# A hybrid encoder block on one core: other PSUM banks, an earlier weight load, another first cast and 16 products moved

## The chip, the cores and the metric

The kernel runs on one core of a Trainium2 chip. TensorE (PE in the profile; PEld is its weight load) does the matmuls into PSUM; VectorE (DVE), ScalarE (ACT) and GpSimd (POOL) do the rest; SyncE (SP) and POOL issue the DMAs. Each engine works through its own instructions in order and waits on semaphores for the others. The metric is the device time of one execution in microseconds (us).

## What is computed

One layer of a streaming encoder over 512 frames of width 1024, in float32:

```
h = rmsnorm(x, norm_mix_g)
a_q, a_k, a_v, b_q, b_f, b_i, b_g, c_q, c_kv, c_kr, gate_logits = split(h @ w_in)
y_a = chunked_relpos_attention(a_q, a_k, a_v, rel_bias)
y_b = hgrn2_recurrence(b_q, b_f, b_i, b_g, lower_bound, norm_g)
y_c = mla_attention(c_q, c_kv, c_kr, positions, ...)
x = x + sum_n(sigmoid(gate_n) * (y_n @ w_branch[n])) @ w_out
h2 = rmsnorm(x, norm_ffn_g)
x = x + square(relu(h2 @ w_ff1)) @ w_ff2
return rmsnorm(x, final_norm_g)
```

Branch C (`mla_attention`) compresses the input to 256 + 128 + 32 columns, normalizes two of the parts, and expands them to queries, keys and values. Branch A has 8 heads of 64 with a relative bias. Branch B is a gated linear recurrence.

## The kernel before

Tensors lie transposed, features on the 128 partitions and the 512 frames along the free axis. Matmuls keep float32 accuracy by splitting both operands into a high half that TensorE takes as it is and a low half, the rest: one product of blocks is three matmuls, high by high, high by low, low by high (`mm3`, `mm3_u`). The norm of the input is applied late: `xg` holds x times the norm's gain, in halves, and each projection is multiplied by `rstd` as it leaves PSUM.

**The start.** `_body` first does eight steps k over 128 rows of x. A step makes the halves of x (ACT L400, VectorE L401), those of the compression weight `w_c` (`split`, L210 and L211), and adds 12 matmuls to four PSUM accumulators `pc` (L224 to L226). The squares of x (ACT L417) are summed by POOL (L419) into `ss`. Then the four accumulators are copied out as `crw` (ACT L427, VectorE L425), squared (L486), and summed over the partitions by matmuls with ones (L490 `pkv`, L491 `pst`, L492 `pq`). From these VectorE and ACT compute the norms (L496 to L506, `rsqrt`), `rstd` among them, and the halves of the normalized compression (`csplit`: `cnh`, `cnl`). The first value blocks `pv` of branch C need these (L635). PSUM has eight banks, given out by tags: `acc` three, `sc` two, `tp` two, `up` one.

**The filler.** While such chains run, TensorE is given matmuls of the large projections from a queue: `project` and `project_nat` add a function each, and `fill(n)` takes n units from it, one matmul of 512 columns each in `project` and on average the same in `project_nat`. TensorE's order is the order of the program (`manual_schedule`); that of the other engines is made by a planner from priorities, in program order, and estimated readiness. `TUNE` holds the sizes of the fills: `s0` ahead of L490, `s1` behind the norms, `c0`, `c1`, `c2`, `ca`, `cb` and `cd` in branch C's preparation, its attention and the attention's drain. The queue of this stage holds the eight blocks of `w_aqk` (24 matmuls each) and the two halves of `w_av`; branch B's projections are added behind the attention (L723).

**The weight loads.** `load` takes the next 512 KB block and issues its DMA on POOL into a buffer of tag `wr` (two buffers) or `wh` (three), by the count of loads so far modulo 5; at most two blocks wait unconverted. `convert` lets ACT write the negated high half to a `wl` buffer (three) and then POOL issues a second DMA of the same block that adds the full weight to it: the low half (L277, L278). `get`, called when a block's first matmul is due, makes sure that two blocks are converted, and asks for the next conversion 12 units later. The compression uses the same buffers: `w_c` comes in through `wr` in four tiles, and its halves lie in `wh` and `wl`, one tile for two steps. At the other end `stream`, for the output projection and the feed-forward part, takes over the three tags.

**Branch C's attention.** `attention` goes through 8 heads by 4 blocks of queries: scores, softmax, transposes two steps later, values; `ca` and `cb` fill between them, and four more rounds without scores drain it. The preparation of branch A's first heads (`prep_a`, L796 to L806) comes behind it in the program.

Of the kernel before, what the change touches and what calls it, by code (L numbers as in the profile page):

```python
# [9 lines left out]
F32 = mybir.dt.float32  # L10
F32R = mybir.dt.float32r
I32 = mybir.dt.int32
AF = mybir.ActivationFunctionType
ALU = mybir.AluOpType
# [3 lines left out]
S = 512  # L18
P = 128
NK = D // P  # L20
# [12 lines left out]
PACE = 12  # L33

TUNE = dict(
    s0=6, s1=30, c0=3, c1=9, c2=18, ca=[5, 3, 3, 1, 3, 3, 3, 5], cb=[1, 0, 3, 5, 3, 1, 4, 4], cd=6, a0=9,
    aa=[7, 0, 6, 4], ab=[4, 2, 7, 5], ad=0, h0=60, ha=[7, 6, 5, 4, 5, 6, 2, 9, 3, 8, 5],
    hb=[8, 8, 5, 7, 6, 6, 5, 2, 20, 5, 4], n0=9,
)
# [99 lines left out]
def _body(ctx, tc, ap, dbgo):  # L139
    nc = tc.nc  # L140
    V, A, G, T = nc.vector, nc.scalar, nc.gpsimd, nc.tensor
# [6 lines left out]
    def f(t):  # L148
        return t.bitcast(F32)
# [7 lines left out]
    act = ctx.enter_context(tc.tile_pool(name="act", bufs=16))  # L157
    ws = ctx.enter_context(tc.tile_pool(name="ws", bufs=3))
# [3 lines left out]
    def acc(n="acc"):  # L162
        return ps.tile([P, S], F32, tag="acc", name=n, bufs=3)

    def pup(n="up"):
        return ps.tile([P, S], F32, tag="up", name=n, bufs=1)
# [4 lines left out]
    def ptp(n="tp"):  # L171
        return ps.tile([P, S], F32, tag="tp", name=n)

    def fqt(n):
        return base.tile([P, S], F32, tag="fq", name=n, bufs=8)
# [19 lines left out]
    ident = base.tile([P, P], F32, name="ident")  # L195
# [13 lines left out]
    def split(hi, lo, src):  # L209
        A.copy(hi, src)  # L210
        V.tensor_tensor(lo, src, f(hi), ALU.subtract)  # L211
# [11 lines left out]
    def mm3(out, wh, wl, xh, xl, start, stop, **kw):  # L223
        T.matmul(out, wh, xh, start=start, stop=False, **kw)  # L224
        T.matmul(out, wh, xl, start=False, stop=False, **kw)  # L225
        T.matmul(out, wl, xh, start=False, stop=stop, **kw)  # L226
# [34 lines left out]
    def load():  # L261

        while loads and len(raw) < 2:
            src = loads.pop(0)
            tag, bufs = (("wr", 2), ("wh", 3))[taken[0] % 5 > 1]
            taken[0] += 1
            hi = ws.tile([P, 1024], F32R, tag=tag, name="wh", bufs=bufs)
            G.dma_start(hi, src)
            raw.append((hi, src))
# [62 lines left out]
    xg = []  # L332
    with ExitStack() as st_ctx:
# [6 lines left out]
            T.matmul(warm[:, :P], ones, ones, start=True, stop=True)  # L340

        xt, wc = [], []
        pc = [acc(f"pc{i}") for i in range(3)] + [pup("pc3")]
        for k in range(NK):
            t = st.tile([P, S], F32, tag="xt", name="xt", bufs=8)
            nc.sync.dma_start(t, ap['xT'][k * P:(k + 1) * P, :])
# [45 lines left out]
                for i in range(first, first + n):  # L392
                    nc.sync.dma_start(dst[16 * i:16 * i + 16, :], d)

        make_identity(nc, ident)
        ss = st.tile([P, S], F32, name="ss")
        for k in range(NK):
            xh = act.tile([P, S], F32R, tag="act", name="xgh")
            xl = act.tile([P, S], F32R, tag="act", name="xgl")
            A.activation(xh, xt[k], AF.Copy, scale=g_mix[:, k:k + 1])  # L400
            V.scalar_tensor_tensor(xl, xt[k], g_mix[:, k:k + 1], f(xh), ALU.mult, ALU.subtract)  # L401
            xg.append((xh, xl))
            j = k % 2
            if j == 0:
                wh = ws.tile([P, 1024], F32R, tag="wh", name="wh")
                wl = ws.tile([P, 1024], F32R, tag="wl", name="wl")
            c = slice(j * 448, (j + 1) * 448)
            split(wh[:, c], wl[:, c], wc[k][:, c])
            for i in range(4):
                m = P if i < 3 else 64  # L410
                c = slice(j * 448 + i * P, j * 448 + i * P + m)
                mm3(pc[i][:m], wh[:, c], wl[:, c], xh, xl, k == 0, k == NK - 1)
            if k == 2:
                rotation = rotary()
            for j in (() if k == 0 else (k - 1,) if k < NK - 1 else (k - 1, k)):
                sq = ss if j == 0 else st.tile([P, S], F32, tag="sq", name="sq", bufs=2)
                A.activation(sq, xt[j], AF.Square)  # L417
                if j:
                    G.tensor_tensor(ss, ss, sq, ALU.add)  # L419
        crw = []  # L420
        for i in range(4):
            t = fqt(f"c{i}")
            m = P if i < 3 else 64
            if i % 2:
                V.tensor_copy(t[:m], pc[i][:m])  # L425
            else:
                A.copy(t[:m], pc[i][:m])  # L427
            crw.append(t)

        def project(src, n, name, out, then=None):  # L430
            def run():
                i = len(out)
                pz = acc("pj")
                yield from gemm_u(pz, get(), xg, NK)
                t = fqt(name)
                V.tensor_tensor(t, pz, rstd, ALU.mult)
                out.append(t)
                if then:
                    then(i, t)
                yield 1  # L440
            for i in range(n):
                last = add([src[i]], run)
            return last

        def project_nat(src, name, pool, out, halves=(0, 1)):

# [21 lines left out]
                last = add([src[half, kk] for kk in range(2)], half_run(half))  # L468
            return last

        aqk, avn, bz, bvn, bq, cums, late = [], [], [], [], [], [], {}
        project(ap['w_aqk'], 8, "aqk", aqk)
        a_done = project_nat(ap['w_av'], "avn", nap, avn)
        convert()
        convert()
# [804 lines left out]
```

## Time and profile before

| | us |
|---|---|
| median of 3 runs | 959.55 (958.98 to 963.6) |
| the profiled execution | 955.7 |
| its span, first to last instruction | 953.9 |
| TensorE busy in it | 915.7 |
| VectorE busy | 595.6 |
| ScalarE busy | 494.5 |
| GpSimd busy | 183.5 |
| granted TensorE clock, mean | 0.995 |

All durations of single instructions come from the profiled execution. A row of its timeline is the start, the length, the engine, the line of the kernel, the instruction with what it writes and reads, and in brackets how long the engine had been idle and who ended that. A row of the waits is who waited for whom, the time in all, how often and the longest. A busy TensorE is not TensorE at its peak: its matmuls overlap, and consecutive ones of 512 columns start about 0.23 us apart.

### The profile page before, as it was taken

The page shows a single profiled execution, that of the slowest core. Times are in us where ns is not written, and L with a number is a line of the kernel's source. Part 1 is how long each engine was busy: PE and PEld are TensorE (multiplying, and loading weights), DVE is VectorE, ACT ScalarE, POOL GpSimd, SP SyncE. Part 2 cuts the span into 40 slices and gives each one's busy share as a digit, 9 for nine tenths or more (in the row PEclk, how much of TensorE's full clock was granted, in tenths as well). Part 3 has the DMA queues.
Part 4 walks back from the last instruction along what each step waited for, and adds up shares of the span by engine and source line. Part 5 has one row for each costly group of instructions (what it writes and reads, how often), then busy time and mean ns, then how long its engine had stood idle before and what let it go on. Part 6 is the DMA issues. An engine that isn't in the chain of part 4 may idle for free.

```text
span 953.9 us, 12608 instructions
## 1 busy us (share of the span) xinstructions
PE 915.7 (96%) x4682; PEld 773.2 (81%) x4682; DVE 595.6 (62%) x1134; ACT 494.5 (52%) x911; POOL 183.5 (19%) x248
## 2 busy tenths in 40 slices
PE   8799999998998999999999999999999999999995
PEld 6578898887877787878788888888888888888994
DVE  6688888787788869788452644544322234446755
ACT  7567778887675767667542434434322233342311
POOL 4422111111163434342122022000000000000032
PEclk9999999999999999999999999999999999999998
DMA  6966445565666564858699532232232322322402
GB/s 201 220 138 125 88 94 112 122 144 116 139 130 135 120 147 91 191 114 179 139 239 194 136 111 89 88 111 89 93 106 88 104 95 89 111 89 91 153 1 89
DMA packets 37181, 117.04 MB, mean 123 GB/s; under 512 B 4416, under 2 KB 8656, under 8 KB 37120
## 3 DMA queue, kind: packets, MB, share of 16 engines
q0 software_dynamic: 18496, 67.17, 33.2%
q1 hardware_dynamic: 18624, 49.06, 15.7%
q8 instruction: 37, 0.61, 0.2%
q14 instruction: 24, 0.20, 0.1%
HBM read 114.05 MB, written 2.16 MB: 122 GB/s over the span
## 4 chain that ended last, share of the span: by engine, by line
PE 71%; DVE 15%; issue 4%; ACT 4%; DMA 3%; POOL 2%; SPq 0%; DVEq 0%; POOLq 0%; ACTq 0%
PE p L226 12%; PE p L225 12%; PE p L224 12%; PE pj L323 3%; PE pj L319 3%; PE pj L321 3%; PE pg L321 2%; PE pg L319 2%; PE pg L323 2%; PE sc L520 2%; DVE qbl L211 2%; PE po L226 2%; PE po L224 2%; PE po L225 2%; DMA bias<-in_rel 2%
## 5 line engine op out<-in xcount | busy, mean ns | idle before, releaser
L220 DVE TENSOR_TENSOR wl<-wr,wh 128x1024 fp32r<-128x1024 f32 x66 | 80.8, 1224 | 145.0 <-ACT wh L219 140.8
L219 ACT CAST wh<-wr 128x1024 fp32r<-128x1024 f32 x66 | 69.5, 1053 | 174.0 <-PE p L225 136.5
L224 PE MATMUL p<-x2h,wh 128*128 128x512 f32 x256 | 100.0, 391 | 0.0
L226 PE MATMUL p<-x2h,wl 128*128 128x512 f32 x256 | 99.6, 389 | 0.0
L225 PE MATMUL p<-x2l,wh 128*128 128x512 f32 x256 | 99.6, 389 | 0.0
L277 ACT ACTIVATE wl<-wh 128x1024 fp32r<-128x1024 f32 x64 | 67.7, 1058 | 47.6 <-PE pg L323 26.4
L224 PE MATMUL p<-rh,wh 128*128 128x512 f32 (+1 forms) x224 | 83.7, 374 | 0.0
L225 PE MATMUL p<-rl,wh 128*128 128x512 f32 (+1 forms) x224 | 83.7, 374 | 0.0
L226 PE MATMUL p<-rh,wl 128*128 128x512 f32 (+1 forms) x224 | 83.7, 374 | 0.0
L1261 POOL TENSOR_TENSOR xres<-xres,cst 128x256 f32<-128x256 f32 x16 | 13.1, 822 | 335.7 <-ACT fss L1256 309.5
L319 PE MATMUL pg<-xgh,wh 128*128 128x512 f32 x192 | 75.7, 394 | 0.3 <-DVE tg L882 0.3
L321 PE MATMUL pg<-xgl,wh 128*128 128x512 f32 x192 | 75.8, 395 | 0.0
L323 PE MATMUL pg<-xgh,wl 128*128 128x512 f32 x192 | 75.6, 394 | 0.0
L319 PE MATMUL pj<-xgh,wh 128*128 128x512 f32 x160 | 64.6, 404 | 2.0 <-ACT c L427 2.0
L321 PE MATMUL pj<-xgl,wh 128*128 128x512 f32 x160 | 65.2, 407 | 0.0
L323 PE MATMUL pj<-xgh,wl 128*128 128x512 f32 x160 | 63.8, 398 | 1.1 <-DMA wl<-in_w_aqk 1.1
L225 PEld LDWEIGHTS p<-x2l,wh 128*128 128x128 f32 x256 | 48.1, 188 | 10.3 <-issue 0.2
L224 PEld LDWEIGHTS p<-x2h,wh 128*128 128x128 f32 x256 | 48.1, 188 | 10.2 <-issue 0.2
L226 PEld LDWEIGHTS p<-x2h,wl 128*128 128x128 f32 x256 | 48.1, 188 | 9.9
L224 PEld LDWEIGHTS p<-rh,wh 128*128 128x128 f32 x224 | 42.2, 188 | 7.5
L225 PEld LDWEIGHTS p<-rl,wh 128*128 128x128 f32 x224 | 42.2, 188 | 7.5
L226 PEld LDWEIGHTS p<-rh,wl 128*128 128x128 f32 x224 | 42.2, 188 | 7.4
(380 smaller groups left out, 2397.4 us busy)
## 6 DMA issues: line engine op xcount, KB each, us to landing
wr<-in_w_ff SPq DMA_DIRECT2D x64, 512.0 KB, 3.3
wh<-in_w_g POOLq DMA_DIRECT2D x24, 512.0 KB, 4.0
wl<-in_w_g POOLq DMA_DIRECT2D x24, 512.0 KB, 6.1
wh<-in_w_br POOLq DMA_DIRECT2D x12, 512.0 KB, 3.6
wl<-in_w_br POOLq DMA_DIRECT2D x12, 512.0 KB, 5.8
wh<-in_w_aqk POOLq DMA_DIRECT2D x8, 512.0 KB, 4.6
wl<-in_w_aqk POOLq DMA_DIRECT2D x8, 512.0 KB, 6.5
wr<-in_w_out SPq DMA_DIRECT2D x8, 512.0 KB, 3.3
```

The lines of the kernel that those rows point to most:

```text
L211: V.tensor_tensor(lo, src, f(hi), ALU.subtract)
L219: A.copy(hi[:, :n], r[:, :n])
L220: (eng or G).tensor_tensor(lo[:, :n], r[:, :n], f(hi[:, :n]), ALU.subtract)
L224: T.matmul(out, wh, xh, start=start, stop=False, **kw)
L225: T.matmul(out, wh, xl, start=False, stop=False, **kw)
L226: T.matmul(out, wl, xh, start=False, stop=stop, **kw)
L277: A.activation(lo, f(hi), AF.Copy, scale=-1.0)
L319: T.matmul(out, wh, xh, start=start, stop=False, **kw)
L321: T.matmul(out, wh, xl, start=False, stop=False, **kw)
L323: T.matmul(out, wl, xh, start=False, stop=stop, **kw)
L520: T.matmul(sc[:, :n], l[:, t * P:(t + 1) * P], r[:, :n], start=i == 0, stop=i == len(scores) - 1)
L1261: G.tensor_tensor(x2[m][:, n], x2[m][:, n], g_fin[:, m:m + 1].to_broadcast([P, 256]), ALU.mult)
```

## The change

Four edits, all in the start:

- Two of the four compression accumulators, `pc1` and `pc2`, go to the tag `tp` instead of `acc`.
- `project` and its lists move up ahead of the loop over k, and at step 6 the loop adds the `w_aqk` projections to the queue and calls `load`, which issues two blocks. Before, they were added behind the loop and first loaded by `convert`. The condition for the tag changes too: of five loads the first three take `wh` and the last two `wr`, where the first two took `wr` and the last three `wh`.
- In step 0 the weight's `split` stands in front of the halves of x. The squares of the first two rows are asked for at step 2 instead of at step 1 and 2.
- `s1` grows from 30 to 46.

```diff
-    s0=6, s1=30, c0=3, c1=9, c2=18, ...
+    s0=6, s1=46, c0=3, c1=9, c2=18, ...
...
-            tag, bufs = (("wr", 2), ("wh", 3))[taken[0] % 5 > 1]
+            tag, bufs = (("wr", 2), ("wh", 3))[taken[0] % 5 < 3]
...
-        pc = [acc(f"pc{i}") for i in range(3)] + [pup("pc3")]
+        pc = [acc("pc0"), ptp("pc1"), ptp("pc2"), pup("pc3")]
...
         for k in range(NK):
             xh = act.tile([P, S], F32R, tag="act", name="xgh")
             xl = act.tile([P, S], F32R, tag="act", name="xgl")
-            A.activation(xh, xt[k], AF.Copy, scale=g_mix[:, k:k + 1])
-            V.scalar_tensor_tensor(xl, xt[k], g_mix[:, k:k + 1], f(xh), ALU.mult, ALU.subtract)
-            xg.append((xh, xl))
             j = k % 2
             if j == 0:
                 wh = ws.tile([P, 1024], F32R, tag="wh", name="wh")
                 wl = ws.tile([P, 1024], F32R, tag="wl", name="wl")
             c = slice(j * 448, (j + 1) * 448)
-            split(wh[:, c], wl[:, c], wc[k][:, c])
+            if k == 0:
+                split(wh[:, c], wl[:, c], wc[k][:, c])
+            A.activation(xh, xt[k], AF.Copy, scale=g_mix[:, k:k + 1])
+            V.scalar_tensor_tensor(xl, xt[k], g_mix[:, k:k + 1], f(xh), ALU.mult, ALU.subtract)
+            xg.append((xh, xl))
+            if k:
+                split(wh[:, c], wl[:, c], wc[k][:, c])
...
             if k == 2:
                 rotation = rotary()
-            for j in (() if k == 0 else (k - 1,) if k < NK - 1 else (k - 1, k)):
+            if k == 6:
+                project(ap['w_aqk'], 8, "aqk", aqk)
+                load()
+            for j in (() if k < 2 else (k - 2, k - 1) if k == 2 else (k - 1,) if k < NK - 1 else (k - 1, k)):
                 sq = ss if j == 0 else st.tile([P, S], F32, tag="sq", name="sq", bufs=2)
...
-        project(ap['w_aqk'], 8, "aqk", aqk)
         a_done = project_nat(ap['w_av'], "avn", nap, avn)
```

More of the change, by code (lines that the diff above doesn't have):

```diff
@@ L35 @@
 TUNE = dict(
-    s0=6, s1=30, c0=3, c1=9, c2=18, ca=[5, 3, 3, 1, 3, 3, 3, 5], cb=[1, 0, 3, 5, 3, 1, 4, 4], cd=6, a0=9,
+    s0=6, s1=46, c0=3, c1=9, c2=18, ca=[5, 3, 3, 1, 3, 3, 3, 5], cb=[1, 0, 3, 5, 3, 1, 4, 4], cd=6, a0=9,
     aa=[7, 0, 6, 4], ab=[4, 2, 7, 5], ad=0, h0=60, ha=[7, 6, 5, 4, 5, 6, 2, 9, 3, 8, 5],
@@ L393, in spread @@
                     nc.sync.dma_start(dst[16 * i:16 * i + 16, :], d)
[L395 to L401, printed above, removed]
-            xg.append((xh, xl))
[L403 to L407, printed above, removed]
-            split(wh[:, c], wl[:, c], wc[k][:, c])
[L409 to L414, printed above, removed]
-            for j in (() if k == 0 else (k - 1,) if k < NK - 1 else (k - 1, k)):
[L416 to L428, printed above, removed]
         def project(src, n, name, out, then=None):
@@ L443, in project @@
             return last
+        make_identity(nc, ident)
+        aqk, avn, bz, bvn, bq, cums, late = [], [], [], [], [], [], {}
+        ss = st.tile([P, S], F32, name="ss")
+        for k in range(NK):
+            xh = act.tile([P, S], F32R, tag="act", name="xgh")
+            xl = act.tile([P, S], F32R, tag="act", name="xgl")
+            j = k % 2
+            if j == 0:
+                wh = ws.tile([P, 1024], F32R, tag="wh", name="wh")
+                wl = ws.tile([P, 1024], F32R, tag="wl", name="wl")
+            c = slice(j * 448, (j + 1) * 448)
+            if k == 0:
[5 more added lines that the diff above has]
+                split(wh[:, c], wl[:, c], wc[k][:, c])
+            for i in range(4):
+                m = P if i < 3 else 64
+                c = slice(j * 448 + i * P, j * 448 + i * P + m)
+                mm3(pc[i][:m], wh[:, c], wl[:, c], xh, xl, k == 0, k == NK - 1)
+            if k == 2:
+                rotation = rotary()
+            if k == 6:
+                project(ap['w_aqk'], 8, "aqk", aqk)
+                load()
+            for j in (() if k < 2 else (k - 2, k - 1) if k == 2 else (k - 1,) if k < NK - 1 else (k - 1, k)):
+                sq = ss if j == 0 else st.tile([P, S], F32, tag="sq", name="sq", bufs=2)
+                A.activation(sq, xt[j], AF.Square)
+                if j:
+                    G.tensor_tensor(ss, ss, sq, ALU.add)
+        crw = []
+        for i in range(4):
+            t = fqt(f"c{i}")
+            m = P if i < 3 else 64
+            if i % 2:
+                V.tensor_copy(t[:m], pc[i][:m])
+            else:
+                A.copy(t[:m], pc[i][:m])
+            crw.append(t)
         def project_nat(src, name, pool, out, halves=(0, 1)):
@@ L469, in project_nat @@
             return last
-        aqk, avn, bz, bvn, bq, cums, late = [], [], [], [], [], [], {}
-        project(ap['w_aqk'], 8, "aqk", aqk)
         a_done = project_nat(ap['w_av'], "avn", nap, avn)
```

## The prediction

> **What bounds the kernel now.** I read the page first, then the waits of TensorE, then the timelines of the start and of the end of the first attention.
>
> ```profile
> span 953.9 us, 12608 instructions
> PE 915.7 (96%) x4682; PEld 773.2 (81%) x4682; DVE 595.6 (62%) x1134; ACT 494.5 (52%) x911; POOL 183.5 (19%) x248
> ```
>
> TensorE is busy for 915.7 of 953.9 us, so a change that leaves its work alone can win only from 38.2 us of gaps. The profiled execution took 955.7 us (the span and 1.8 us around it). The sum below is made against it; the median of the runs shown, 959.55, lies 3.9 us higher, and the gain is subtracted from both. What a measurement of this kernel can tell from no change is about 0.5%, 4.8 us.
>
> TensorE's timeline of the start has the gaps that the change aims at (start, length, engine, line, instruction; in brackets the idle time before it and who ended it):
>
> ```profile
> 6.78 0.50 PE L224 MATMUL pc<-xgh,wh 128*128 128x512 f32 x1 [0.83 <-ACT wh L210]
> ...
> 8.10 0.50 PE L226 MATMUL pc<-xgh,wl 128*128 128x512 f32 x1 [0.44 <-DVE wl L211]
> ...
> 30.27 0.39 PE L226 MATMUL pc<-xgh,wl 128*64 128x512 f32 x1
> 32.63 0.49 PE L319 MATMUL pj<-xgh,wh 128*128 128x512 f32 x1 [1.97 <-ACT c L427]
> ...
> 34.45 0.50 PE L323 MATMUL pj<-xgh,wl 128*128 128x512 f32 x1 [1.09 <-DMA wl<-in_w_aqk]
> ...
> 35.48 1.02 PE L490 MATMUL pkv<-csq,ones 128*128 128x512 f32 x2
> ...
> 37.65 0.79 PE L319 MATMUL pj<-xgh,wh 128*128 128x512 f32 x1
> ...
> 46.13 0.50 PE L224 MATMUL pv<-cwh,cnh 128*128 128x512 f32 x1 [1.09 <-ACT cnh L210]
> ...
> 48.47 0.50 PE L226 MATMUL pv<-cwh,cnl 128*128 128x512 f32 x1 [1.61 <-DVE cnl L211]
> 48.81 0.39 PE L319 MATMUL pj<-xgh,wh 128*128 128x512 f32 x1
> ```
>
> The reader is to see four gaps between the end of the compression (30.5) and 48.5: 1.97, 1.09, 1.09 and 1.61, together 5.8 us. The first is a bank, the second a weight, the last two wait for the norms. With what the first matmul can gain, that is the most that the start can give.
>
> **Step 1: the first cast.** ACT and VectorE at the start:
>
> ```profile
> 5.03 0.72 ACT L400 ACTIVATE xgh<-xt,cst 128x512 fp32r<-128x512 f32 x1 [3.01 <-DMA cst<-in_cst]
> 5.66 0.61 ACT L417 ACTIVATE ss<-xt 128x512 f32<-128x512 f32 x1
> 6.18 0.55 ACT L210 CAST wh<-wr 128x448 fp32r<-128x448 f32 x1
> ...
> 6.37 0.75 DVE L401 SCALAR_TENSOR_TENSOR xgl<-xt,cst,xgh 128x512 fp32r<-128x512 f32 x1
> ```
>
> A copy and a square stand in front of the weight cast. With the cast in the 3 us that ACT idles, the first matmul could start at 5.75, 1.0 us sooner. The second needs xgl, ready at 7.1 as now, but the weight's low half, which VectorE makes behind xgl, could be done in front of it; then the third product comes at about 7.4 instead of 8.10. Bounds 0 (ACT's order is the planner's, and it may keep copy and square in front) to 1.0; I take 0.7, the third product's: the compression ends at 29.8. The squares go one step back; their sum is wanted only at L491, after all of this, so 0.
>
> **Step 2: the banks.** The 1.97 us were pj waiting for an acc bank: ACT copies pc0 out only after a conversion that had itself waited 3.53 us.
>
> ```profile
> 31.05 1.06 ACT L277 ACTIVATE wl<-wh 128x1024 fp32r<-128x1024 f32 x1 [3.53 <-DMA wh<-in_w_aqk]
> 32.01 1.06 ACT L427 COPY c<-pc 128x512 f32<-128x512 f32 x2
> ```
>
> With pc1 and pc2 in the tp banks, two acc banks are free and this wait is gone. Late next is the weight.
>
> **Step 3: the loads.** POOL issues them now so; below it the times from issue to landing, of the high halves issued up to 70 us and of the low halves up to 75 us:
>
> ```profile
> 20.43 1.34 POOL L419 TENSOR_TENSOR ss<-ss,sq 128x512 f32<-128x512 f32 x1 [6.66 <-DMA dcos<-cs]
> 21.72 0.56 POOL L268 DMA_DIRECT2D wh<-in_w_aqk  x1
> ...
> 23.53 0.56 POOL L268 DMA_DIRECT2D wh<-in_w_aqk  x1
> ...
> 28.62 0.94 POOL L278 DMA_DIRECT2D wl<-in_w_aqk  x1
> ```
>
> ```profile
> DMA to landing us min/median/max: 3.6/4.5/9.5
> ```
>
> ```profile
> DMA to landing us min/median/max: 5.7/6.7/9.1
> ```
>
> The cadence of products comes from one row of the output projection: 64 instructions of one of three kinds, so 189 steps from 545.5 to 588.3, 0.226 us each.
>
> ```profile
> L224 PE MATMUL po<-mh,wh x64: 389/389/389, 545.5 to 588.3; 128*128 128x512 f32 x64
> ```
>
> One compression step is 12 products, 2.7 us; counted back from 30.5, step 3 ends at 19.6, and 0.7 sooner after the first cast. The first load now goes into the buffer of steps 2 and 3, at about 19 instead of 21.72, in POOL's idle time; the two loads then stand in front of sums of squares, which wait 0.56 us for each, and for the buffer if TensorE is late: no cost, since those sums are wanted at L491. The first high half lands 4.5 later, is negated (1.06), and its low half is issued at about 25.5, where now it goes at 28.62. That one landed at 34.45, 5.8 later; so it lands at 31.3. TensorE does two products from 29.8 and waits 1.0 us. The six products end at 32.2 (31.3 and four more) instead of 35.48, 3.3 sooner; bounds: 31.2 (no wait) and 35.4 (low half as now).
>
> VectorE's norm chain starts after the three sums and ends with cnl, 11.0 us later:
>
> ```profile
> 37.40 0.69 DVE L496 TENSOR_SCALAR vx<-pst 128x512 f32<-128x512 f32 x1 [1.73 <-PE pst L491]
> ...
> 47.75 0.67 DVE L211 TENSOR_TENSOR cnl<-c,cnh 128x512 fp32r<-128x512 f32 x1
> ```
>
> It starts 1.9 after the six products: from 34.1 to 45.1, instead of 48.4.
>
> **Step 4: 46 products.** They start 2.2 after the six (35.48 to 37.65), at 34.4, and take 46 x 0.226 = 10.4: to 44.8. They cover the chain. But 6 + 46 = 52 products need a third weight block, where 36 needed two, and its low half is wanted at the 51st, 44.4. The new count of buffers gives the third block the slot of compression steps 6 and 7, free only at 29.8; now it goes into an earlier slot (the row at 23.53). From 29.8: 0.1 to issue, 4.5 to 9.5 to land, 1.06 to negate, 0.1, 6.7 to 9.1 to land: ready at 42.3 to 49.7. I take 7.0 and 7.9, the middles, because the DMA engines are full there (the last columns are granted clock, DMA share, GB/s):
>
> ```profile
> 32.00:34.00 2.00, 0.73 (x2) 0.30 (x2) 0.00 (x0) 1.97 (x5) 1.60 (x3) 1.00 1.03 231
> ...
> 40.00:42.00 2.00, 2.00 (x11) 1.65 (x10) 0.32 (x1) 2.00 (x4) 0.00 (x0) 1.00 1.11 270
> ```
>
> That is 46.0: TensorE waits 1.6 us at the 51st product, ends the 52nd at 46.4 and the first value block's three pv matmuls at 47.1, where now it is through at 48.8. Behind this wait stands, in TensorE's fixed order, the whole first attention. The start gives **1.7 us**; bounds +3.3 (weight in time, cnl at 45.1 sets the end) and -2.0 (ready at 49.7). The gap moves from the norms to a weight.
>
> The Trainium skill ("DMA: Bandwidth & Descriptors", Anatomy of one DMA, SWDGE path) fits such a transfer with 2.0 us plus bytes at 436 GB/s: as an estimate, 3.2 us for 512 KB. By it the third block would be ready at 37.5 and the start would give the 3.3. The medians measured here are longer than that, so the measurement decides.
>
> **Step 5: where the 16 products are taken from.** The filler queue of this stage holds 8 x 24 + 2 x 48 = 288 units. Ahead of the drain the code asks for 6 + 30 + 12 + 45 + 104 + 84 = 281 now and for 297 after: nine units of the last step and the seven of the drain go. In the trace these are the 33 half-width pv products of the window 152.6 to 158.6 (length, TensorE busy and count, clock, DMA), 3.7 us at the cadence. Below it TensorE and VectorE behind the last scores:
>
> ```profile
> 152.60:158.60 6.00, 4.59 (x33) 1.00 0.54 94
> ```
>
> ```profile
> 159.18 0.66 PE L545 MATMUL tp<-ident,p 128*128 128x128 f32 x4 [0.63 <-DVE pTl L211]
> ...
> 162.34 0.45 PE L319 MATMUL pj<-xgh,wh 128*128 128x512 f32 x1
> ```
>
> ```profile
> 154.18 0.69 DVE L797 SCALAR_TENSOR_TENSOR qt<-aqk,qt 64x512 fp32r<-64x512 f32 x1
> 154.90 0.69 DVE L525 TENSOR_REDUCE mn<-sc 128x1 f32<-128x512 f32 x1
> ...
> 160.49 0.69 DVE L211 TENSOR_TENSOR pTl<-tp,pTh 128x512 fp32r<-128x512 f32 x1 [0.90 <-ACT pTh L210]
> ```
>
> Taking 3.7 us of filler away doesn't end the stage 3.7 us sooner: TensorE waits for VectorE there already, and VectorE's rows have no idle bracket until the 0.90. Bounds: 0 (VectorE's order stays) to 3.4 (the 0.90 goes, and the preparations for the next attention that stand between, four like the 0.69 at most, yield). I take **0.9**: a gap goes, the order stays.
>
> **Step 6: the far end of the buffer count.** 64 blocks are loaded; the last has a wh buffer now and a wr buffer after. So the second raw block of the output projection can load only when the gates end, at 545.
>
> ```profile
> L220 DVE TENSOR_TENSOR wl<-wr,wh 128x1024 fp32r<-128x1024 f32 x66 | 80.8, 1224 | 145.0 <-ACT wh L219 140.8
> L219 ACT CAST wh<-wr 128x1024 fp32r<-128x1024 f32 x66 | 69.5, 1053 | 174.0 <-PE p L225 136.5
> ...
> wr<-in_w_out SPq DMA_DIRECT2D x8, 512.0 KB, 3.3
> ```
>
> 3.3 + 1.05 + 1.22 = 5.6 us, against 24 products and two, 5.9: 0, at worst 0.6 for issue and queues.
>
> Sum: 1.7 + 0.9 + 0 = 2.6 us. 955.7 becomes 953.1, the median 959.55 becomes **957.0**.
>
> **The rivals.** *In time* (0.22): the third block lands at the median times and VectorE's preparations yield: 3.3 + 3.4 = 6.7 us, 952.9. For it: every load but this one can go sooner. Against: the full DMA engines. The skill's transfer time would give this too. *ACT blocked* (0.12), slower: the planner puts the third block's negation in front of the norm chain's first logarithm,
>
> ```profile
> 39.31 0.63 ACT L240 ACTIVATE st_l<-vk 128x512 f32<-128x512 f32 x1 [3.58 <-DVE vk L498]
> ```
>
> as it now puts the second one's in front of L427 with 3.53 us of waiting. If the block lands 9.5 after 29.9, at 39.4, ACT is free at 40.5, and the logarithm, due 3.3 sooner than now at 36.0, is 4.5 late: cnl at 49.6, the low half at 49.7, or at 51.0 if POOL is held up by a sum like the 1.34 above. Then pv ends at 52.1, 3.3 us later than now; with nothing from the tail, 962.9. It costs from a low half later than 47.7 on; before that the start still gains. *The order stays* (0.16): the planner keeps cast and conversions where they are, the low half lands at 34.4, the six products end at 35.4 as now and the chain at 48.4; the 16 products fill gaps that the chain keeps open: 0.1 + 0.9, 958.6.
>
> **How the numbers follow.** Forecast 0.50, in time 0.22, order stays 0.16, ACT blocked 0.12. Faster by over 0.5% is the second case, 0.22. Slower by over 0.5% (964.4) needs the fourth at its worst with step 6, or an order of the planner that I don't see: 0.07. The rest, 0.71, is within 0.5%. The sum's ends are 6.7 gained (952.9) and 2.6 lost (962.2); the range cuts the upper a little: 953.0 to 961.5. Outside lie most of ACT blocked and the edge of in time.
>
> **What would show it.** Right: no wait for L427 at 30; a pj wait on wl of about a microsecond at the third product and another at the 51st; pv's L226 no longer waiting for cnl; no pv products after the last scores, with longer gaps in front of L545 and L561; the next attention's first product at about 160 instead of 162.3. Wrong: no wait on wl near 45 (the third block is faster than I think), L277 with a long wait in front of L240, or differences behind 165 us, where only buffers and the planner's order change; a shift of some microseconds there is not in my sum.

## The result, and the profile after

The changed kernel takes 966.48 us (median of 7 runs, 964.87 to 967.88) where the kernel before takes 959.55 (7 runs, 957.63 to 963.62): ratio 1.0059, 95% interval 1.0040 to 1.0078. It is slower by 0.6%; the forecast was 957.0, the range 953.0 to 961.5.

The profiled execution of the changed kernel took 967.9 us, 12.2 more than the one before. That is more than the 6.9 between the medians: the execution profiled before, 955.7, lies below all seven timed runs of its kernel. The head of the changed kernel's page:

```profile
span 966.1 us, 12612 instructions
PE 923.0 (96%) x4682; PEld 778.6 (81%) x4682; DVE 596.7 (62%) x1134; ACT 494.3 (51%) x911; POOL 183.9 (19%) x248
```

TensorE does the same 4682 instructions and is busy 7.3 us longer: part of the time it runs at a lower clock. Below, its two longest waits (total, times, longest), then its timeline of the start. Behind the loop, lines of the changed kernel lie some five further than before.

```profile
PE pj L323 <- DMA wl<-in_w_aqk: 6.3, 1, 6.3
PE tp L550 <- DVE pTl L211: 5.1, 4, 3.2
```

```profile
30.41 0.39 PE L226 MATMUL pc<-xgh,wl 128*64 128x512 f32 x1
30.64 0.39 PE L319 MATMUL pj<-xgh,wh 128*128 128x512 f32 x1
30.87 0.40 PE L321 MATMUL pj<-xgl,wh 128*128 128x512 f32 x1
37.58 0.79 PE L323 MATMUL pj<-xgh,wl 128*128 128x512 f32 x1 [6.32 <-DMA wl<-in_w_aqk]
...
42.61 0.79 PE L319 MATMUL pj<-xgh,wh 128*128 128x512 f32 x1
...
53.45 0.39 PE L224 MATMUL pv<-cwh,cnh 128*128 128x512 f32 x1
...
54.14 0.40 PE L321 MATMUL pj<-xgl,wh 128*128 128x512 f32 x1
```

The wait for the bank is gone: the projection starts at 30.64, right behind the compression. In its place stands one wait of 6.32 us for the first low half. The first value block of branch C is through at 54.14, where it was at 48.81. Why the low half came no sooner stands on POOL:

```profile
20.60 1.34 POOL L441 TENSOR_TENSOR ss<-ss,sq 128x512 f32<-128x512 f32 x1 [6.66 <-DMA dcos<-cs]
21.89 1.10 POOL L268 DMA_DIRECT2D wh<-in_w_aqk  x2
...
26.31 0.55 POOL L268 DMA_DIRECT2D wh<-in_w_aqk  x1 [2.00 <-DVE wl L211]
...
28.12 0.56 POOL L268 DMA_DIRECT2D wh<-in_w_aqk  x1
...
29.95 0.93 POOL L278 DMA_DIRECT2D wl<-in_w_aqk  x1
```

The load that the change asks for two steps sooner still stands behind a sum of squares for which POOL idles 6.66 us; two loads go from 21.89 on (before, one at 21.72). The first of the two lands at 26.3, but ScalarE, idle by then, begins the first negation only when the second has landed, 6.0 us after its issue. The first negation in the changed kernel, then in the kernel before:

```profile
28.50 1.06 ACT L277 ACTIVATE wl<-wh 128x1024 fp32r<-128x1024 f32 x1 [3.52 <-DMA wh<-in_w_aqk]
```

```profile
26.46 1.06 ACT L277 ACTIVATE wl<-wh 128x1024 fp32r<-128x1024 f32 x1 [1.69 <-DMA wh<-in_w_aqk]
```

So the block that is converted first is the second to be loaded. Four high halves, where there were three, precede its low half, which goes at 29.95 (before 28.62) and takes 7.6 us to land (before 5.8).

Behind the start the profiles are easiest compared stage by stage. "Start" is from the sum `pst` over the partitions to C's first scores, "attention" from there to its last scores, "drain 1" on to the last group of transposes (`tp`, x4), "drain 2" on to A's first scores, "rest" on to the first product of the output projection. All are differences of starts in TensorE's timeline, in us.

| run | pst at | start | attention | drain 1 | drain 2 | rest | ratio to before (95%) |
|---|---|---|---|---|---|---|---|
| before | 36.3 | 31.8 | 83.8 | 7.3 | 5.3 | 381.0 | 1 |
| before, again (e12) | 37.5 | 33.4 | 83.7 | 7.3 | 5.3 | 382.5 | |
| banks alone (e3) | 39.7 | 31.9 | 83.7 | 7.3 | 5.3 | 381.0 | 0.9999 (0.9985 to 1.0012) |
| new count alone (e4) | 41.4 | 31.1 | 83.7 | 7.3 | 6.9 | 383.6 | 1.0020 (1.0004 to 1.0035) |
| s1=46 alone (e5) | 39.0 | 33.1 | 86.0 | 6.5 | 8.4 | 379.7 | 1.0051 (1.0032 to 1.0071) |
| **after** | 41.2 | 32.4 | 86.0 | 6.5 | 8.6 | 383.1 | 1.0059 (1.0040 to 1.0078) |
| after, old count (e1) | 38.3 | 33.2 | 86.0 | 6.5 | 8.4 | 383.7 | 1.0051 (1.0034 to 1.0068) |
| after, s1=30 (e2) | 41.2 | 30.3 | 83.7 | 7.3 | 5.3 | 383.8 | 1.0002 (0.9985 to 1.0019) |
| after, s1=38 (e10) | 42.0 | 31.6 | 85.7 | 6.2 | 8.2 | 383.0 | 1.0035 (1.0012 to 1.0058) |

The sum of the parts from the profile before to the one after: 4.8 until `pst`, 0.6, 2.2, -0.8, 3.3, 2.1: 12.2. The first two and the last of these also differ between the two profiles of one and the same kernel (by 1.1, 1.6 and 1.4 us), or between kernels with the same program there. In the rows with `s1` at 30 and at 46, attention and drain 1 go with it to a tenth of a microsecond. Drain 2 goes with it to two tenths, but for e4 (and e8, below), where it takes 6.9 us with `s1` at 30: the granted clock falls there too, though TensorE has its filler and no wait in front is longer than 0.68 us. In e4 (the columns are explained further below; 0.56 is the clock):

```profile
166.00:168.00 2.00, 2.00 (x9) 1.82 (x8) 1.16 (x2) 1.78 (x4) 0.85 (x1) 0.56 0.43 94
```

### The profile page after: what moved, and what is told of

It is laid out like the page before. It is cut to its first block, busy times and chain, and to the rows that moved or that the text cites. A ratio compares the mean times of both kernels' runs of the same rounds, so it can differ in the third digit from the quotient of the medians.

```text
span 966.1 us, 12612 instructions
## 1 busy us (share of the span) xinstructions
PE 923.0 (96%) x4682; PEld 778.6 (81%) x4682; DVE 596.7 (62%) x1134; ACT 494.3 (51%) x911; POOL 183.9 (19%) x248
## 4 chain that ended last, share of the span: by engine, by line
PE 69%; DVE 13%; issue 8%; DMA 4%; ACT 3%; POOL 2%; SPq 0%; DVEq 0%; POOLq 0%; ACTq 0%
PE p L225 12%; PE p L224 12%; PE p L226 12%; PE pj L323 3%; PE pj L319 3%; PE pj L321 3%; PE pg L323 3%; PE pg L319 3%; PE pg L321 3%; DMA bias<-in_rel 2%; PE po L225 2%; PE po L226 2%; PE sc L525 2%; PE po L224 2%; DVE qbl L211 1%
## 5 line engine op out<-in xcount | busy, mean ns | idle before, releaser
L224 PE MATMUL p<-rh,wh 128*128 128x512 f32 (+1 forms) x224 | 83.7, 374 | 0.0
L225 PE MATMUL p<-rl,wh 128*128 128x512 f32 (+1 forms) x224 | 83.7, 374 | 0.0
L226 PE MATMUL p<-rh,wl 128*128 128x512 f32 (+1 forms) x224 | 83.7, 374 | 0.0
```

## The experiments

Theory 1: the new count of buffers puts high halves ahead of the first low half, TensorE idles, and loses its clock. Theory 2: the price is that of the 16 products taken from the drain. Theory 3: banks, first cast or early load. Two more came up on the way: theory 4, that the waits within the attention depend on where a weight conversion falls, and theory 5, that POOL holds VectorE there.

**One part undone, one part alone.** In the changed kernel the old count (e1) and the old `s1` (e2); in the kernel before the banks (e3) and the new count (e4).

```diff
 e1, on the changed kernel
-            tag, bufs = (("wr", 2), ("wh", 3))[taken[0] % 5 < 3]
+            tag, bufs = (("wr", 2), ("wh", 3))[taken[0] % 5 > 1]
 e2, on the changed kernel
-    s1=46
+    s1=30
 e3, on the kernel before
-        pc = [acc(f"pc{i}") for i in range(3)] + [pup("pc3")]
+        pc = [acc("pc0"), ptp("pc1"), ptp("pc2"), pup("pc3")]
 e4, on the kernel before
-            tag, bufs = (("wr", 2), ("wh", 3))[taken[0] % 5 > 1]
+            tag, bufs = (("wr", 2), ("wh", 3))[taken[0] % 5 < 3]
```

> The changed kernel with the old rule of the buffer count (blocks 1 and 2 of the projection into wr, 3 to 5 into wh); banks, early load, first cast and s1=46 stay. Theory 1 (the new count puts high halves of blocks that are needed late, in wr, ahead of the first low half on POOL's queue): the wait of the projection's third product for wl falls from 6.32 us to under 2.5, the granted clock after it stays at 1.00, A's end comes 5 to 8 us sooner than in the changed kernel: ratio to before 0.998 to 1.002. Theory 2 (the 16 products taken out of the tail and the half clock there are the greater part): wait gone or not, ratio still 1.004 or more. Theory 3 (banks, first cast or the early load itself): wait of 6 us stays, ratio 1.005 to 1.007.

> The changed kernel with s1=30 in place of 46; all else as changed. Theory 1: the wait of 6.3 us for the first low half stays, the 30 products end some 3 us ahead of the norm chain (51.3) and TensorE waits there instead; the tail gets its 16 products back: ratio 1.003 to 1.007. Theory 2: the tail's idle 3.2 us and its 4 us at half clock go, last scores of C to A's first product back at about 10.4 us with 3.7 us of products in it: ratio 1.000 to 1.003.

> The kernel before with the accumulators of the compression in the new banks alone. Theories 1 and 2: the projection's first product starts 2 us sooner (about 30.6), the third still waits for the low half that lands at 34.4: ratio 0.999 to 1.001. Theory 3 in its form with the banks as cause: a longer wait somewhere in the first 60 us, ratio 1.003 or more.

> The kernel before with the new rule of the buffer count alone (blocks 1 to 3 into wh, 4 and 5 into wr). Theory 1: more high halves ahead of the first low half on POOL's queue, low half 2 us or more later than 34.45, TensorE idle over 3 us there and at a lower granted clock after it: ratio 1.003 to 1.008. Theories 2 and 3: ratio 0.999 to 1.001.

Theory 1 had the cause of the wait nearly right and the price wrong. The new count is what puts the first negation off: it begins at 28.50 to 29.03 in the changed kernel, e2 and e4, and at 26.46 and 26.55 in the kernel before and in e1. In e1 the low half is issued at 27.91, the wait falls to 2.90 us (expected: under 2.5; the clock falls to 0.50 even so), `pst` comes 2.9 us sooner, and the ratio is 1.0051 all the same. In e2 the wait is 5.75 us, and the kernel is as quick as before: 1.0002. So by the medians 0.57% of the 0.59% go with `s1`. e3 gave nothing, as the first two theories wanted; its profile shows how loose one wait is. POOL issues the first low half at 28.64, as in the profile before (28.62), and it lands 7.6 us later instead of 5.8:

```profile
36.20 0.74 PE L323 MATMUL pj<-xgh,wl 128*128 128x512 f32 x1 [5.10 <-DMA wl<-in_w_aqk]
```

In e4 the wait is 5.34 us and the clock falls behind it, as theory 1 said, but the ratio, 1.0020, lies between what the theories wanted. Its interval overlaps e2's, so whether the count costs something by itself isn't shown.

**The 16 products in the kernel before (e5).** As in e2, with 46 on the kernel before.

> The kernel before with s1=46 alone. Theory 2 (the 16 products are missing behind the last scores of C, where TensorE then idles over 3 us and runs at a lower granted clock for some microseconds): an idle of about 3.2 us in front of the transposes of the drain, granted clock below 0.8 in the 10 us behind it, last scores of C to first scores of A 14.5 to 15 us instead of 12.5; ratio 1.002 to 1.006. Rival (the 16 products cost only together with the early load or the new buffer count): ratio 0.998 to 1.001.

Theory 2's numbers, all of them: 1.0051, the drain 14.9 us instead of 12.5. Nothing else of the change is needed for the loss. That the loss arises in the drain isn't shown by this: the attention is 2.2 us longer as well.

**Where do they cost?** e2 and the changed kernel have the same `pst` (41.19 and 41.16), so their profiles are the best pair to subtract: start +2.1, attention +2.2, drain 1 -0.8, drain 2 +3.3: 6.8, where the medians differ by 5.7. The start is the loosest of these, since it differs by 1.6 us between the two profiles of the kernel before.

*Start.* In e2 the 30 products end ahead of the norm chain; VectorE's low half `cnl` is done at 51.40. In the changed kernel it is done at 51.30:

```profile
42.35 0.69 DVE L501 TENSOR_SCALAR vx<-pst 128x512 f32<-128x512 f32 x1 [5.50 <-PE pst L496]
...
50.61 0.69 DVE L211 TENSOR_TENSOR cnl<-c,cnh 128x512 fp32r<-128x512 f32 x1 [0.28 <-ACT cnh L210]
```

The chain takes 8.95 us and 46 products take 10.84 (42.61 to 53.45). They cover it and run on for 2.15 us. From `pst` to the end of the first value block it takes 12.98 us, in e2 10.61: of the 16 products' 3.6 us (at 0.226 each) 2.4 find no gap to fill.

*Attention.* Between 95 and 132 the waits of TensorE list nothing in e2 and two in the changed kernel, 1.1 for `qt` and 0.9 for `p`. VectorE's sum of the rotated queries, and POOL at the same time, in the changed kernel, then in e2:

```profile
114.63 2.79 DVE L700 TENSOR_TENSOR qr<-qr,qr 64x512 f32<-64x512 f32 x1
```

```profile
114.42 0.86 POOL L278 DMA_DIRECT2D wl<-in_w_av  x1 [0.77 <-ACT wl L277]
114.99 1.88 POOL L631 TENSOR_TENSOR cwl<-cwr,cwh 128x640 fp32r<-128x640 f32 x1
```

```profile
112.44 1.29 DVE L700 TENSOR_TENSOR qr<-qr,qr 64x512 f32<-64x512 f32 x1
```

```profile
111.63 1.55 POOL L631 TENSOR_TENSOR cwl<-cwr,cwh 128x640 fp32r<-128x640 f32 x1 [3.67 <-ACT cwh L630]
```

The sum ends 0.55 us behind POOL's subtraction in both (117.42 and 116.87; 113.73 and 113.18), as if it stood still meanwhile; e11, below, puts that to the test. With 46, the conversions, which are counted in filler units, fall in front of the subtraction and move it onto the sum. All eight profiles with 46 and POOL's subtraction show 2.79 or 2.80 there, and none with 30 or 38 shows over 1.42. The Trainium skill ("SBUF — State Buffer", SBUF: two separate sides) says that VectorE, when it reads two operands from SBUF, and GpSimd lock a port pair for a whole instruction and the other blocks; the 0.55 us behind the end in both cases agree. By the Trainium skill the one that starts first has the ports; in the changed kernel the sum's record starts 0.36 us ahead of the subtraction's and still ends last, which no run here explains (a DMA issue of POOL, at 114.42, is ahead of both).

*Drain.* Of each kernel the last transposes, the first values, the first of nine products and A's first scores; the changed kernel, then e2:

```profile
166.02 1.12 PE L550 MATMUL tp<-ident,p 128*128 128x128 f32 x4 [3.21 <-DVE pTl L211]
167.81 0.79 PE L566 MATMUL av<-pTh,v 128*128 128x512 f32 x1 [0.68 <-ACT pTh L210]
...
170.63 0.73 PE L319 MATMUL pj<-xgh,wh 128*128 128x512 f32 x1
...
174.57 0.33 PE L525 MATMUL sc<-kt,qt 128*128 128x128 f32 x2
```

```profile
162.52 0.66 PE L550 MATMUL tp<-ident,p 128*128 128x128 f32 x4 [0.61 <-DVE pTl L211]
163.86 0.49 PE L566 MATMUL av<-pTh,v 128*128 128x512 f32 x1 [0.67 <-ACT pTh L210]
...
165.67 0.45 PE L319 MATMUL pj<-xgh,wh 128*128 128x512 f32 x1
...
167.80 0.33 PE L525 MATMUL sc<-kt,qt 128*128 128x128 f32 x2
```

Without its filler TensorE reaches the last transposes only 0.8 us sooner: it waits 3.21 us for VectorE. After that the same instructions take 8.55 us instead of 5.28. The windows of the changed kernel (length, TensorE busy, weight loads, VectorE, ACT, POOL, then the granted clock, DMA share and GB/s) show a clock of 0.50 there:

```profile
162.00:164.00 2.00, 0.52 (x3) 0.31 (x3) 1.81 (x4) 1.93 (x4) 0.00 (x0) 1.00 0.50 180
...
168.00:170.00 2.00, 1.95 (x5) 1.34 (x6) 1.29 (x2) 0.87 (x2) 0.00 (x0) 0.50 0.85 106
...
172.00:174.00 2.00, 2.00 (x6) 1.59 (x5) 1.53 (x3) 0.49 (x1) 0.00 (x0) 0.50 0.00 0
```

**Is the clock in the drain part of the price?** e6, e13 and e15 put useless matmuls into the drain, e7 real ones.

```diff
 e6: two at each of eight places; e13: six at the two places ahead of the last transposes; e15: four more behind them
+        spare = psc("spare") if dum else None
+        def idle(n):
+            for _ in range(n):
+                T.matmul(spare, xg[0][0][:, :P], xg[0][0], start=True, stop=True)
...
+            idle(i >= len(order) and dum)
 e7
-    cd=6
+    cd=2
...
+            project(ap['w_bq'][0:1], 1, "bq", bq)
             attention(ab, lambda h: ready(h % 2), next_c, v2, pT, ys, TUNE['ca'], TUNE['cb'], TUNE['cd'])
...
-            else:
+            elif i:
                 b_done = project(ap['w_bq'][i:i + 1], 1, "bq", bq)
```

> The changed kernel with 16 extra matmuls of 512 columns in the drain of C's attention, two at each of its eight places, whose result is never read (3.6 us of useless work at full clock). Theory 2, with the clock as the price: the idle in front of the transposes falls below 1.5 us, the clock stays at 1.00 there, last scores of C to first scores of A about 12.5 us instead of 14.8; ratio 1.001 to 1.004 although TensorE does more. Rival (the drain takes as long as VectorE's chain, the clock is only a companion): 14.8 us as in the changed kernel or longer, ratio 1.005 to 1.008.

> The changed kernel with one block of branch B's projection (24 products of w_bq) put into the queue ahead of C's attention instead of behind it, and cd=2, so that some 15 real products stand in the drain again. Theory 2: clock 1.00 in the drain, 12.5 us from last scores of C to first scores of A, ratio 0.999 to 1.002 (as without the 16, or a little better, since these products are then missing nowhere). Rival (16 products ahead of C's attention cost by themselves): ratio 1.004 or more.

> The changed kernel with 12 extra matmuls of 512 columns whose result is never read, all of them between the second last and the last transposes of C's drain, where TensorE otherwise idles 3.21 us (12 take 2.7 us); behind the last transposes nothing is added, other than in the run with 16. Theory 2, clock as the price: granted clock 1.00 from there on, the last transposes start at the same distance from the last scores (6.5 us), the values and nine products behind them take 5.3 us instead of 8.55, A's first scores 3 us sooner; ratio 1.002 to 1.004. Rival (what is gained there is lost in A's attention, which VectorE sets): A's first scores 3 us sooner in the profile, ratio 1.005 to 1.007.

> As the run with 12 extra matmuls ahead of the last transposes of C's drain, and 4 more right behind them, where TensorE idled 1.79 us and then 0.33 and the clock fell again. Theory 2: granted clock 1.00 through to A's first scores; last transposes to A's first scores 6.5 us or less instead of 8.55 (the changed kernel) and 9.3 (the run with 12); A's first scores 2 us sooner after C's last scores than in the changed kernel (13 instead of 15); ratio 1.002 to 1.004. Rival (nothing in the drain matters for the end, or the clock falls anyway): ratio 1.005 to 1.007.

| run | last scores of C to first of A, us | ratio (95%) |
|---|---|---|
| after | 15.06 | 1.0059 (1.0040 to 1.0078) |
| e6 | 13.74 | 1.0065 (1.0043 to 1.0087) |
| e7 | 14.45 | 1.0044 (1.0024 to 1.0063) |
| e13 | 15.80 | 1.0051 (1.0029 to 1.0073) |
| e15 | 13.10 | 1.0057 (1.0038 to 1.0077) |

In e6 the idle time in front of the transposes was still 2.27 us, but the clock held; half of its matmuls lie behind the transposes. In e13 the first idle time was filled, and the clock fell all the same, behind a second one of 1.79 us. In e15 it held, in the same microseconds as above:

```profile
168.00:170.00 2.00, 1.23 (x5) 0.86 (x6) 1.19 (x2) 0.46 (x2) 0.00 (x0) 1.00 0.79 127
```

In the profile, A's first scores come 2 us sooner, as expected; in the times nothing comes of it, against the expectation. A gain of 2 us would be 1.0038, the edge of e15's interval, and e6 is no better. It isn't that the profile misleads: the mean granted clock, which is on record for each timed run, is 0.986 over the seven of the changed kernel and 0.989 over the six of e15, as over the twelve of e2. So the timed runs of e15 have less half clock too, and no gain is seen (over the twelve of e6 it is only 0.987). The half clock's share of the measured 0.57% is not shown. In e7, with real products in the drain, the clock stays at 1.00 as well, but the drain takes 14.45 us and not 12.5, and the ratio is the rival's; it isn't told apart from the changed kernel either.

**Is the attention's wait a matter of place, and is POOL its cause?** e10 takes half of the step, s1=38. e11 lets VectorE make the low halves `cwl`.

```diff
 e11, on the changed kernel, in cweights
-                G.tensor_tensor(lo[:, :n], r[:, :n], f(hi[:, :n]), ALU.subtract)
+                V.tensor_tensor(lo[:, :n], r[:, :n], f(hi[:, :n]), ALU.subtract)
```

> The changed kernel with s1=38, half of the step from 30 to 46. Theory 4 (the 2.0 us that TensorE waits in C's attention at 118 to 124 come from where a weight conversion and a block's end happen to fall, since the fill counts set it): the VectorE sum of the rotated queries takes 0.7 to 1.3 us in all four heads instead of 2.8 in one, no waits of 1.1 and 0.9 us there; of the price of s1=46 only the drain's is left; ratio 1.000 to 1.003. Rival (the price grows evenly with the number of products moved): ratio 1.003 to 1.004, with half of each loss in the trace.

> The changed kernel with the low halves of branch C's weights (cwl, five subtractions) made by VectorE instead of POOL. Theory 5 (VectorE's sum of the rotated queries stands still while POOL subtracts, 2.79 us instead of 0.7): that sum takes 0.7 in all four heads, the waits for qt and p at 118 to 124 go or fall below 0.5 us, last scores of C to first scores of C shorter by 1.5 to 2.0 us than the changed kernel's 85.9; VectorE does 3 to 4 us more in all, beside TensorE; ratio 1.003 to 1.005. Rival (the sum is long for another reason, or VectorE's extra work takes its place): waits of 1 us or more stay, ratio 1.005 to 1.008.

Theory 4 fell: at 38 the sum takes 1.30 us, but the attention is 85.7 us long by other waits (0.93 for `p` at 99, 0.53 for `avn` at 144), and the ratio, 1.0035, is the rival's half. Theory 5 held for the sum. It takes 0.68 in all heads:

```profile
115.72 0.68 DVE L700 TENSOR_TENSOR qr<-qr,qr 64x512 f32<-64x512 f32 x1
```

Of the 2.0 us of waits 0.3 are left, the attention is 1.4 us shorter (a little under the 1.5 expected), the ratio 1.0033 (1.0018 to 1.0049); this interval overlaps the changed kernel's, so the gain in time is likely and not sure.

**How far one profile carries (e12).** The kernel before, unchanged.

> The kernel before, another profiled execution. All theories: the same order of instructions; what is open is the time from issue to landing of the first low half, 5.8 us in the first profile and 7.6 in the kernel with new banks alone. If it is 5.8 again, the banks change the landing; if it is over 7, one profile of each kernel doesn't show which is the usual case, and the third product's wait is no price of the change.

The low half lands 5.8 us after its issue again (29.75 to 35.56). That doesn't make the 7.6 of e3 a matter of the banks, as the expectation had it: the landing takes 6.9 us in e5, which has the old banks, and from 5.4 (e15) to 7.6 in the eight profiles that start as the changed kernel does. This profile's compression ends at 34.6, four microseconds later than in the first, though `pst`, which waits for the low half, only 1.1 later. What comes late is the DMA of the positions (`rpi`). VectorE's cast of them, in the first profile and in e12, stands ahead of the first low half of x:

```profile
6.26 0.20 DVE L366 CAST ang<-rpi 128x64 f32<-128x64 int32 x1 [1.06 <-DMA rpi<-in_pos]
```

```profile
7.48 0.20 DVE L366 CAST ang<-rpi 128x64 f32<-128x64 int32 x1 [2.38 <-DMA rpi<-in_pos]
```

In e12 the third product then starts at 10.41 instead of 8.10, and the granted clock is 0.50 to 0.74 from 8 to 16 us, where it was 1.00. The cast is as late in the profiles of e10 and e16. No run puts it elsewhere, so what that would give is open.

**Can the start be mended?** e8, with s1=30: all 16 products with the high half ahead of the 8 with the low half, in the first block. e9 adds an order on ScalarE and VectorE, e14 adds e11's edit to e9, e16 puts `s1` back to 46 in e9.

```diff
 e8, in gemm_u, for the first block of aqk
+            for low in (0, 1):
+                for k in range(nk):
+                    c = slice(k * cols + off, k * cols + off + P)
+                    for x in ((acts[k][0],) if low else acts[k]):
+                        T.matmul(out, w[low][:, c], x, start=..., stop=...)
 e9, besides
-            A.activation(lo, f(hi), AF.Copy, scale=-1.0)
+            i = A.activation(lo, f(hi), AF.Copy, scale=-1.0)
+            if hold[0] is not None:
+                after(i, hold[0])
...
         convert()
-        convert()
         spread(rotation)
...
         V.tensor_tensor(csq[1], csq[1], csq[2], ALU.add)
+        convert()
...
         rq = rsqrt(stt, vq)
+        hold[0] = sqs[-1]
...
+            with urgent():
                 ckv = [csplit(crw[2])]
                 cqn = [csplit(t) for t in crw[:2]]
...
-            for a in (slice(32, 64), slice(64, 128)):
-                V.tensor_scalar(sinT[a], sinT[a], sgn[a], None, ALU.mult)
...
+            for a in (slice(32, 64), slice(64, 128)):
+                after(V.tensor_scalar(sinT[a], sinT[a], sgn[a], None, ALU.mult), splits[-1])
```

`after` sets only an order. At the second `convert`, `hold[0]` is the last square of the compression; `sqs` and `splits` collect the norms' squares and VectorE's halves of `split`. Lines of e8 and e9 lie 10 to 17 further than in the changed kernel.

> The changed kernel with s1=30, and in the first block of the projection all 16 products with the high half ahead of the 8 with the low half (the same 24 products into the same bank). Theory 1 (the wait for the first low half and the clock behind it cost the start 3 to 5 us): the six products ahead of the norms need no low half, the sums over the partitions come at 32 to 33 instead of 41, the wait for wl falls below 1.5 us, first scores of C at 66 to 68 instead of 71.5; ratio 0.994 to 0.998. Rival (what the start gains is lost again in a later stage): first scores as early, ratio 0.999 to 1.002.

> As the run with the high halves first (s1=30), and besides an order put on ScalarE and VectorE: the second block's negation behind the squares of the compression, the later ones behind the norm chain's last square, the cast of the normalized compression ahead of other work, VectorE's products with sinT's sign behind that. Theory 1 (ScalarE's in-order waits for weights in front of the copies, the squares and the first logarithm are what the start loses once the products no longer wait): no wait of 2.9 us in front of the sums over the partitions, these at 32 to 34 instead of 35 to 39, granted clock 0.9 or more from 30 to 50, the first scores of C at 64 to 66 instead of 69.8; ratio 0.992 to 0.996. Rival (weights then arrive too late for TensorE and the gain is a wait for wl): first scores at 68 or later, ratio 0.997 to 1.001.

> The run with the order on ScalarE and VectorE (s1=30, high halves first), and besides the low halves of branch C's weights made by VectorE instead of POOL. Theory 5: VectorE's sums of the rotated queries take 0.7 instead of 1.3 us, but TensorE didn't wait for them at s1=30, so nothing is gained: ratio 0.994 to 0.997, as without it. Rival (POOL, freed of the first subtraction at 30.5, issues loads sooner, and wl lands sooner): the wait of 2.7 us for wl falls below 1.5, ratio 0.991 to 0.994.

> The run with the order on ScalarE and VectorE and the high halves first, with s1=46 as in the change instead of 30. Its start no longer waits for the first low half. Theory 2 (the 16 products cost where they are missing and where they are added, whatever the start does): first value block of C 3.5 us later than with 30, since at 30 there is no wait for the norms to cover; idle of about 3 us in the drain; ratio 0.999 to 1.003, some 5 us over the run with 30. Rival (they cost because the start was late): ratio 0.995 to 0.998.

e8 fell short, 0.9987 (0.9968 to 1.0005): the products no longer wait for the low half, but the sums over the partitions and the logarithm do, by way of ScalarE, where the planner sets negations that wait for a DMA in front of ready work:

```profile
32.57 1.06 ACT L277 ACTIVATE wl<-wh 128x1024 fp32r<-128x1024 f32 x1 [2.89 <-DMA wh<-in_w_aqk]
33.53 0.57 ACT L459 COPY c<-pc 128x512 f32<-128x512 f32 x1
34.13 1.67 ACT L501 ACTIVATE csq<-c 128x512 f32<-128x512 f32 x3
41.98 1.06 ACT L277 ACTIVATE wl<-wh 128x1024 fp32r<-128x1024 f32 x1 [6.17 <-DMA wh<-in_w_aqk]
42.94 0.62 ACT L240 ACTIVATE st_l<-vk 128x512 f32<-128x512 f32 x1
```

The logarithm's input `vk` had been ready since 40.5. That is the prediction's rival of the blocked ScalarE; it didn't come about in the changed kernel only because there `vk` was late itself (44.2). In e9 the sums start 0.2 us behind the six products:

```profile
31.10 0.40 PE L336 MATMUL pj<-xgl,wh 128*128 128x512 f32 x1
31.34 1.02 PE L510 MATMUL pkv<-csq,ones 128*128 128x512 f32 x2
32.20 1.02 PE L511 MATMUL pst<-ss,ones 128*128 128x512 f32 x2
...
37.06 2.12 PE L336 MATMUL pj<-xgh,wl 128*128 128x512 f32 x8 [0.71 <-DMA wl<-in_w_aqk]
```

`pst` at 32.2 (after: 41.2), C's first scores at 64.8 (after: 73.6); the ratio is 0.9954 (0.9935 to 0.9972), 957.13 us against 961.30 for the kernel before in the same series. Theory 1's numbers came out here, but e9 changes three orders at once and no run parts them. e14 is the quickest, 954.41 us against 960.78, 0.9927 (0.9898 to 0.9955), faster than both kernels; its interval doesn't part it from e9. Its ratio is the rival's, but the wait for `wl` is 2.2 us, not below 1.5, so what it may gain over e9 isn't the rival's sooner weight. e16 loses all of it again, 1.0020 (1.0002 to 1.0038), as theory 2 expected: start +3.1, attention +2.2, drain +2.4 against e9. In its profile another 4.7 us lie ahead of `pst`, where the cast of the positions was late; the medians, 5.0 us apart, say better than this profile what the 16 products cost with this order.

## Why the prediction was wrong, step by step

- **What bounds the kernel**: right in kind (four gaps, each of which went or moved), but the sum was made as if the gaps of the start could be had without the planner's order.
- **Step 1**, 0.7: came out at its lower bound, 0: the order stayed, as the step's own condition for 0 had it. ScalarE still does copy, square, cast at 5.12, 5.75, 6.27, and the first product starts at 6.87.
- **Step 2**: right, and worth nothing (0.9999), since the weight is late next, as the step said.
- **Step 3**: failed first. "At about 19 instead of 21.72, in POOL's idle time" took the idle time for free; it lies behind a waiting sum on an in-order queue. It also let the first high half land 4.5 us after that; but with the new count another block is loaded ahead of it, and its negation began at 28.50, where the step has it end at 24.6 (19 + 4.5 + 1.06; the 25.5 that it goes on with holds 0.9 more that it doesn't name). The low half came at 37.58 instead of 31.3, and the six products ended at 39.45, outside the bounds of 31.2 to 35.4, which held no later issue and no longer landing. Yet this isn't what made the kernel slower (e2).
- **Step 4**: the mechanism was turned round. The third block was in time and the 46 products cover the chain, but the step rested on a chain of 11.0 us. It took 8.95, and VectorE had four pieces of work less in front of `cnl`. The products ran 2.15 us past it. "The start gives 1.7" became a first value block 5.3 later: 4.8 of it lie ahead of `pst`, where one profile is loose; behind it the shorter chain gave 1.9 (from `pst` to the block's end 12.47 before, 10.61 in e2) and the 16 products took 2.4 (12.98).
- **Step 5**: the size came out near, to the last transposes (0.9 said, 0.8 measured), but by luck. The gap of 0.90 lies behind those transposes, and VectorE's order did not stay: from the last scores on, two of the four preparations no longer stand in front, and VectorE waits 1.05 us for ScalarE where it hadn't. This is the step that failed for the time: it counts what the 16 products free in the drain, 0.9, and puts what they bring about elsewhere at nothing. They shift the weight conversions through the attention, which lost 2.2 us (e11 takes 1.4 of them away), and leave TensorE idle for 3.21 us, behind which the profile shows 3.3 us more, at half the clock. Neither was a term of the sum or a rival. In place of a gain of 2.6 us the runs show a loss of 0.5 to 0.6% that goes with these 16 products alone (e2, e5).
- **Step 6**: 0, right: from the first to the last product of the output projection both take 42.8 us.
- **Rivals**: "the order stays" came nearest in the start, but gave the 16 products a gap to fill; "ACT blocked" was seen in e8, not here. What was slower was a mechanism that none of them named, and 0.07 for it was too little.

What stays open: how the measured 0.57% of `s1` divides. Start and attention account for 4.3 us in the profile; e11's 0.26% in the times would be most of the second, but the intervals overlap. The drain's second part is 3.3 us in the profile, and holding up the clock there shows no gain in the times of e6 and e15.

## What to carry to other kernels

Filler moved from one gap to another costs what it is longer than the new gap (here some 2.4 of 3.6 us), and pays back only what the engine that set the old gap allows: compare both gaps before moving it, and don't read the moved work as free in either. An earlier request is earlier only if the in-order queue in front of it isn't waiting, so it can pay to order waits for a DMA behind ready work by hand (here 0.9987 became 0.9954, together with two other changes of order). And where conversions are paced by counted units, a changed count moves them against everything behind it; look for the stage where they collide.

## What the hardware showed that I had not expected

- VectorE's addition of two SBUF operands, 0.68 us alone (e11), took 1.3 and 2.79 us beside a subtraction on POOL and ended 0.55 us behind it each time.
- The granted clock fell to 0.50 behind idle times of 6.3, 3.2 and, in e13, 1.8 us, and came back about 4, 8 and 7 us after work resumed; in the profile before, gaps of 1.97 and 1.09 close to each other left it at 1.00, and in e4's drain it fell behind waits of 0.62, 0.68 and 0.23, which in the same place left it at 1.00 in the kernel before. The Trainium skill ("TensorE: Matmul & The Clock Gate", Part 1) lets the clock fall after at least one idle window of about 3.4 us. The gap of 6.3 us agrees with that; the falls behind the shorter ones it doesn't explain.
- The same low half took 5.8 us from issue to landing in two profiles of the kernel before and 7.6 in e3, issued in the same order, and from 5.4 to 7.6 among eight profiles with one and the same start.
